# A hybrid attention layer on one core: the dilated heads' output projection moved into the latent stage, its sums passed through DRAM

## Chip, core and metric

One core of one Trainium2 chip. The metric is the device time of one execution in microseconds; the lower the better. Times inside a profiled execution are counted from the start of its span.

## What is computed

One decoder layer on x of 1024 positions by 1024 channels, float32. One input projection gives latent queries and keys, gates, and the dilated heads' q, k and v. Eight latent (MLA) heads of 64 and eight dilated heads of 64 each give a 512-wide output per position; each is multiplied by a SiLU gate. The part that matters here is the end:

```python
y_a = mla_attention(c_q, c_kv, k_rope, q_norm_g, kv_norm_g, w_uq, w_ukv) * jax.nn.silu(g_a)
y_b = dilated_attention(q_b, k_b, v_b) * jax.nn.silu(g_b)
mix = jnp.concatenate([y_a, y_b], axis=-1)
x = layernorm(DEEPNORM_ALPHA * x + mix @ w_out, ln_g, ln_b)
```

`mix @ w_out` contracts 1024 channels: blocks 0 to 3 of 128 are the latent heads' pairs, blocks 4 to 7 the dilated heads' pairs.

## The kernel before

Matrices with float32 precision are split into a high and a low part (`hi_lo`, L74: a ScalarE copy in the matmul's float32 format, then a subtraction on VectorE or GpSimd), and each product takes three passes: high by high, high by low, low by high (`PASSES`, L36). Code is written in program order; a scheduler of the framework orders each engine's queue, and tile pools decide when a buffer is free. Each engine and each DMA queue works through its instructions in that order. Loads, stores and transposing DMAs are issued by SyncE (SP).

The stages, by the time they take place:

1. Input projections, splits and their stores to DRAM (to about 290 us).
2. The dilated heads, pair by pair (L591 to L687), with the gates' matmuls (`gate`, L517) as fillers between them. The gated result of pair j and half s of the positions is the tile `GT[4 + j, s]`, 128 channels by 512 positions.
3. The latent heads (L962 to L1007). The loop runs over 64 units: 4 pairs `hp`, in each 4 chunks `ch` of 256 positions (in the order of `CHS`), 2 heads `e` and 2 blocks `qi` of 128 queries. A unit is: `scores` (L789, three passes of a 128-query block against its 128 to 1024 keys into a PSUM tile S, then VectorE's scale, mask and minimum, L810), `expo` (ScalarE, L815), and three units later `inverse`, `high` (L823: for some widths a scaling on GpSimd, then ScalarE's rounding to f16) and `low` (L835: the rest, on GpSimd or VectorE, and a DMA that transposes the probabilities into PT, L844). Eight units later `values` (L846) multiplies with V and VectorE gates the result into GT (L857). The next pair's keys (`gen_k`, L723) and queries (`gen_q`, L761) are made in between. PSUM: scores have three tiles of two banks; `values`, `gen_k` and `gen_q` share the pool `pb` of two banks (`gbank`, L582).
4. The output projection. `KORD` (L921) is the order of the eight blocks: 0, 1, 4, 5, 6, 7, 2, 3. `load_wo` (L926) loads and splits a block's 128 x 1024 weights, `load_y` (L938) splits the gated results. Blocks 0 and 1 of three rows of 128 positions are begun during pair 3; four more weight blocks (`LATE`, L961) and the rest are loaded around the last units, into buffers of the pools that units use (`b4`, `hp_`). `project` (L948) does 6 matmuls of 512 columns per block and row into PSUM: 48 per row, 384 in all.
5. Row by row `residual` and `finish` (L1036 to L1061), all on VectorE but for one square root: x times ALPHA plus the sum (L1041), statistics (L1044, L1049), 1 / sqrt refined by a Newton step (L1051 to L1056), and two steps with the gain and the shift (L1059, L1060), then the store.

The last stage of a row in the kernel before:

```python
nc.vector.scalar_tensor_tensor(x[:, a:b], x[:, a:b], ALPHA, p[:, a:b], ALU.mult, ALU.add)      # L1041
nc.vector.scalar_tensor_tensor(o, o, mv[:, 0:1], lg[c], ALU.subtract, ALU.mult)                # L1059
nc.vector.scalar_tensor_tensor(o, o, rs[:, 1:2], lb[c], ALU.mult, ALU.add)                     # L1060
```

Line numbers L... are those of the kernel before unless said otherwise; the new code stands some 7 to 50 lines further down (its chunk matmuls are its L986, its residual additions L1084, its shift additions L1111).

## Time and profile before

| what | us |
|---|---|
| median of 3 runs (lowest, highest) | 653.2 (651.88, 655.94) |
| the profiled execution | 648.14 |
| its span, first to last instruction | 646.3 |
| TensorE busy in the span | 594.8 |
| VectorE busy | 398.2 |
| ScalarE busy | 320.0 |
| GpSimd busy | 299.1 |

The span is 1.84 us shorter than the execution's time. Busy times of TensorE count a matmul from its start to its modelled end, and matmuls overlap, so two busy matmuls in a row can stand for less work than the sum of their durations. PEclk in a window is the granted TensorE clock as a share of its higher level (2.4 GHz; the lower, 1.2 GHz, would be 0.50).

### The profile page before, as it was taken

What the parts mean: (1) busy time and instruction counts of PE and PEld (TensorE: products, weight loads), DVE (VectorE), ACT (ScalarE), POOL (GpSimd) and SP (SyncE); (2) the same over time, 40 slices, a digit from 0 to 9 for tenths busy, and PEclk for the clock granted to TensorE, in tenths of its full rate; (3) what the DMA queues carried; (4) which work ended last, traced back from release to release, by engine and by line L of the source; (5) the groups of instructions that cost most, each with busy time, mean ns of one, the idle gap of its engine ahead of it and who ended that gap; (6) DMA issues with size and microseconds to landing.
All of it is one profiled execution on the core that took longest, in us unless ns stands there. A gap on an engine that the chain in (4) does not pass through costs nothing. (4 is left out here: it accounts for less than half of the span.)

```text
span 646.3 us, 11099 instructions
## 1 busy us (share of the span) xinstructions
PE 594.8 (92%) x4046; PEld 435.7 (67%) x4046; DVE 398.2 (62%) x890; ACT 320.0 (50%) x645; POOL 299.1 (46%) x326
## 2 busy tenths in 40 slices
PE   8999998999999899999997987887989977999995
PEld 5888886788999366776764644434545546778884
DVE  3425318480541686644644897678898997365696
ACT  4452136554221386545636575577978787340000
POOL 3374754265331227534644757373758566450000
PEclk9999999999999999999997997988999987999999
DMA  6666137796012779993999996549798899752042
GB/s 198 188 198 198 30 97 204 221 289 174 33 66 74 260 233 144 184 208 78 225 296 234 184 212 147 108 94 185 150 159 163 173 199 225 185 154 81 17 163 98
DMA packets 198663, 105.52 MB, mean 163 GB/s; under 512 B 157520, under 2 KB 175568, under 8 KB 198480
## 3 DMA queue, kind: packets, MB, share of 16 engines
q1 hardware_dynamic: 195008, 99.11, 64.7%
q10 hardware_dynamic: 3600, 5.71, 3.4%
q8 instruction: 31, 0.51, 0.3%
q14 instruction: 24, 0.20, 0.1%
HBM read 47.65 MB, written 18.35 MB: 102 GB/s over the span
## 5 line engine op out<-in xcount | busy, mean ns | idle before, releaser
L522 PE MATMUL gP<-x,wg 128*128 128x512 f32 x384 | 98.8, 406 | 5.9 <-ACT wg L75 5.5
L522 PEld LDWEIGHTS gP<-x,wg 128*128 128x128 f32 x384 | 70.7, 191 | 23.2 <-ACT wg L75 6.1
L953 PE MATMUL op<-wo,ys 128*128 128x512 f32 x288 | 70.7, 401 | 0.6 <-ACT ys L75 0.4
L953 PEld LDWEIGHTS op<-wo,ys 128*128 128x128 f32 x288 | 54.3, 191 | 14.4 <-ACT ys L75 0.9
L815 ACT ACTIVATE p<-p,sm 128x128 f32<-128x128 f32 (+3 forms) x64 | 49.1, 767 | 22.1 <-DVE sm L810 17.3
L804 PE MATMUL S<-k,q 128*128 128x512 f16 (+3 forms) x288 | 54.7, 339 | 5.2 <-DVE sm L810 4.8
L253 PE MATMUL cP<-x,wc 128*128 128x512 f32 x240 | 56.7, 395 | 0.0
L810 DVE CUSTOM_DVE_ANT_0 p<-S,mask,fs 128x128 f32<-128x128 f32 (+3 forms) x64 | 50.5, 809 | 4.7 <-POOL ph L840 3.4
L253 PEld LDWEIGHTS cP<-x,wc 128*128 128x128 f32 x240 | 44.7, 188 | 10.3
L620 ACT ACTIVATE td<-td,st 128x384 f32<-128x384 f32 (+1 forms) x64 | 42.1, 659 | 16.6 <-DVE st L614 16.4
L638 POOL TENSOR_SCALAR td<-td,st 128x384 f32<-128x384 f32 (+1 forms) x32 | 22.5, 710 | 56.9 <-DVE st L626 44.4
L804 PEld LDWEIGHTS <-q 128*128 128x128 f16 x288 | 26.7, 101 | 30.8 <-issue 5.7
L614 DVE CUSTOM_DVE_ANT_0 td<-Sd,mdil,dsc 128x384 f32<-128x384 f32 (+1 forms) x64 | 41.3, 679 | 9.1 <-PE Sd L610 8.9
L168 PE MATMUL acc<-wq,x 128*128 128x512 f32 x192 | 45.1, 395 | 0.9 <-DVE x L155 0.8
L854 PE MATMUL O<-pT,v 128*64 128x256 f16 (+1 forms) x480 | 33.1, 285 | 13.9 <-DMA pT<-ph 11.4
L129 PE MATMUL qkP<-wk,x 128*128 128x512 f32 x192 | 44.5, 393 | 0.0
L840 POOL TENSOR_TENSOR ph<-p,ph 128x256 f16<-128x256 f32 (+3 forms) x32 | 36.6, 1153 | 15.6 <-ACT ph L833 12.4
L854 PEld LDWEIGHTS <-v 128*64 128x64 f16 x480 | 28.8, 119 | 22.1 <-issue 18.4
L842 DVE SCALAR_TENSOR_TENSOR ph<-p,sm,ph 128x128 f16<-128x128 f32 (+3 forms) x32 | 35.0, 1101 | 13.8 <-ACT ph L833 13.8
L168 PEld LDWEIGHTS acc<-wq,x 128*128 128x128 f32 x192 | 36.0, 188 | 10.5 <-DVE x L155 1.3
L129 PEld LDWEIGHTS qkP<-wk,x 128*128 128x128 f32 x192 | 36.0, 188 | 8.2
L653 POOL TENSOR_TENSOR p<-td,p 128x384 f16<-128x384 f32 (+1 forms) x32 | 35.7, 1124 | 11.4 <-ACT p L643 11.2
(313 smaller groups left out, 1158.7 us busy)
## 6 DMA issues: line engine op xcount, KB each, us to landing
u<-in_w_u_dram SPq DMA_DIRECT2D x20, 256.0 KB, 3.1
v_d<-v SPq DMA_DIRECT2D x16, 256.0 KB, 2.1
wor<-in_w_o_dram SPq DMA_DIRECT2D x8, 512.0 KB, 4.2
xr<-in_xres_dram SPq DMA_DIRECT2D x16, 256.0 KB, 3.1
out_dram<-xr SPq DMA_DIRECT2D x16, 256.0 KB, 2.1
xr<-in_xT_dram SPq DMA_DIRECT2D x15, 256.0 KB, 3.0
k_d<-k SPq DMA_DIRECT2D x8, 384.0 KB, 4.4
c_d<-c SPq DMA_DIRECT2D x10, 256.0 KB, 2.4
```

Source lines behind the costliest of these rows:

```text
L129: nc.tensor.matmul(d, xs[k][i // 4][:, a, (i % 4) * P:(i % 4) * P + P], w8[k][:, b, o:o + w], **flags(k, KD, (a, b)))
L168: nc.tensor.matmul(acc[i], xs[k][i // 4][:, a, (i % 4) * P:(i % 4) * P + P], ws[:, b, :512], start=(k == 0 and (a, b) == (0, 0)), stop=(k ...
L253: nc.tensor.matmul(dst, ww(k, a, m), xs[k][s][:, b], **flags(k, KD, (a, b)))
L522: nc.tensor.matmul(p, wg[k // 4][:, a, (k % 4) * P:(k % 4) * P + P], xs[k][s][:, b], **flags(k, KD, (a, b)))
L614: nc.vector.tensor_tensor_reduce(TD[u_][:, e, :ns * P], S[e], mk, dsc[:, 1:2], BIG, ALU.add, ALU.min, stt[:, e, 0:1])
L620: nc.scalar.activation(t[:, :w], t[:, :w], AF.Exp, bias=ST[u_][:, e, 0:1], scale=-1.0, accum_out=ST[u_][:, e, 1:2])
L804: nc.tensor.matmul(S[:, lo:hi], q[:, a, qc], k[:, b, lo:hi], start=((a, b) == (0, 0)), stop=((a, b) == (1, 0)))
L810: nc.vector.tensor_tensor_reduce(t[:, :w], S[:, :w], M["mask"][:, T - w:], fs[:, 7:8], BIG, ALU.add, ALU.min, sm[:, 0:1])
L815: nc.scalar.activation(TT[u][:, :w], TT[u][:, :w], AF.Exp, bias=SM[u][:, 0:1], scale=-1.0, accum_out=SM[u][:, 1:2])
L840: nc.gpsimd.tensor_sub(p16[:, :, 1], t, p16[:, :, 0])
L854: nc.tensor.matmul(O[ME[e], q0:], V[hp][:, kb, vh, ME[e]], rhs, **flags(kb, 2 * ch + 2, (vh, phl)))
L953: nc.tensor.matmul(op[i][:, half(c)], ys[k][a][:, i * P:(i + 1) * P], ws[k][b][:, half(c)], **flags(n_, KD, (a, b)))
```

## The change

- The four dilated blocks of the projection become a generator, `project_dilated`: for each of two halves s of the positions and two halves c of the output columns, four weight pieces of 128 x 512 are loaded (three of the four times), split, and, the first time in s, the gated results too; then for each of four rows 12 matmuls go into one bank of `pb`, a ScalarE copy evicts it, and a store writes it to the DRAM tile `part_d`. That is 16 chunks; each is advanced by half a chunk in two of three units from unit 1 to 47, so beside pairs 0 to 2.
- `KORD` is now 0, 1, 2, 3; blocks 0 to 2 get their weights during pair 3, block 3 after the last unit. Three rows are begun before the last values.
- In the last stage each row's x is multiplied by ALPHA on ScalarE and the stored sum is added on GpSimd (`load_x`); VectorE adds PSUM. For the first five rows the normalisation is one ScalarE instruction (scale and bias), a product with the gain on GpSimd and an addition of the shift on VectorE; the last three rows keep the two steps on VectorE.
- GT tiles are allocated in one place; the second key pair K[1] lies in another pool; new pools `pw` (4), `ph` (5), `pr` (1), `pe` (1) take the room.

```diff
-    KORD = (0, 1, 4, 5, 6, 7, 2, 3)
+    KORD = (0, 1, 2, 3)
...
+        M["pw"], M["ph"], M["pr"], M["pe"] = r("pw", 4), r("ph", 5), r("pr"), r("pe")
...
+    def project_dilated():
+        wd, hi, lo = {}, {}, {}
+        for s, c in ((0, 0), (0, 1), (1, 1), (1, 0)):
+            for j in range(4):
+                if (s, c) != (1, 1):
+                    r = M["pr"].tile([P, 512], F32, name=f"pr{j}{s}{c}", tag="r")
+                    sync.dma_start(r, w_o[4 + j, :, half(c)])
+                    wd[j] = M["pw"].tile([P, 2, 512], F32R, name=f"pw{j}{s}{c}", tag="w")
+                    hi_lo(wd[j][:, 0], wd[j][:, 1], r, nc.gpsimd)
+                if s == c:
+                    g = GT[4 + j, s]
+                    hi[j] = M["ph"].tile([P, 512], F32R, name=f"ph{j}{s}", tag="h")
+                    p_, t_ = (gy, "g") if j + s else (M["ph"], "h")
+                    lo[j] = p_.tile([P, 512], F32R, name=f"pl{j}{s}", tag=t_)
+                    hi_lo(hi[j], lo[j], g, nc.gpsimd)
+            for i in range(4):
+                p = gbank(f"pd{s}{c}{i}")
+                for j in range(4):
+                    for a, b in PASSES:
+                        y = (hi, lo)[a][j]
+                        nc.tensor.matmul(p, y[:, i * P:i * P + P], wd[j][:, b], **flags(j, 4, (a, b)))
+                    if j == 1:
+                        yield
+                t = M["pe"].tile([P, 512], F32, name=f"pe{s}{c}{i}", tag="e")
+                nc.scalar.copy(t, p)
+                sync.dma_start(part_d[4 * s + i, :, half(c)], t)
+                yield
...
-    DR = {3: [0, 1], 5: [2, 3], 7: [4, 5]}
-    NW, NWS, NYS = 2, 4, 3
-    LOADW, LOADY, PROJ0, NY = (3, 8), (5, 8, 10), (13, 15), 3
-    LATE = (NU - 2, NU, NU + 1, NU + 5)
+    DR = {3: [0, 1], 5: [2]}
+    NW, NY = 3, 3
+    LOADW, LOADY, PROJ0 = (3, 5, 8), (5, 8, 10), (13, 15)
+    more = project_dilated()
...
+        if n < 48 and n % 3 or n == 47:
+            next(more, None)
+        if n == NU:
+            load_wo(KORD[3], b4, "b")
...
+    load_y(KORD[3], hp_, "p16")
...
+        t = (b4 if j < 4 else rows).tile([P, T], F32, name=f"row{i}", tag="b" if j < 4 else "row")
+        sync.dma_start(t, part_d[i])
+        for c in range(2):
+            nc.scalar.mul(xr[i][c], xr[i][c], ALPHA)
+            nc.gpsimd.tensor_add(xr[i][c], xr[i][c], t[:, half(c)])
...
-        nc.vector.scalar_tensor_tensor(x[:, a:b], x[:, a:b], ALPHA, p[:, a:b], ALU.mult, ALU.add)
+        nc.vector.tensor_add(x[:, a:b], x[:, a:b], p[:, a:b])
...
+        last = i in ROWS[-3:]
+        if not last:
+            nc.vector.scalar_tensor_tensor(rs[:, 0:1], mv[:, 0:1], -1.0, rs[:, 1:2], ALU.mult, ALU.mult)
...
+                nc.scalar.activation(o, o, AF.Identity, scale=rs[:, 1:2], bias=rs[:, 0:1])
+                nc.gpsimd.tensor_mul(o, o, lg[c])
+                nc.vector.tensor_add(o, o, lb[c])
```

What the new order of instructions is at three places follows. TensorE, pair 1, around the second query projection of head 1 (`qg111`), before: the scores of unit (1, 0, head 1, block 0), then the query projection.

```order
L804 MATMUL S101_5063<-k11_4060,q101_4950 128x128
L804 LDWEIGHTS q101_4950
L804 MATMUL S101_5063<-k11_4060,q101_4950 128x128
L765 LDWEIGHTS u1_4792
L765 MATMUL qg111_5074<-c2_3662,u1_4792 128x512
```

And now: between scores and the same projection stand the last matmuls of two chunks, `pd010` and `pd011`, both of the second group of weights, for their fourth weight piece (`pw301`; `ph30` and `pl30` are the high and low part of the gated result).

```order
L811 LDWEIGHTS q101_5063
L811 MATMUL S121_5345<-k11_4699,q101_5063 128x384
L986 MATMUL pd010_5101<-pw301_5098,ph30_4765 128x512
L986 MATMUL pd011_5200<-pw301_5098,ph30_4765 128x512
L986 MATMUL pd010_5101<-pw301_5098,ph30_4765 128x512
L986 MATMUL pd010_5101<-pw301_5098,pl30_4766 128x512
L986 MATMUL pd011_5200<-pw301_5098,ph30_4765 128x512
L986 MATMUL pd011_5200<-pw301_5098,pl30_4766 128x512
L772 LDWEIGHTS u1_4873
L772 MATMUL qg111_5239<-c2_3666,u1_4873 128x512
```

The query projection has moved behind both chunks, which hold the two banks of `pb` until the fourth piece is there, and the scores have run one chunk further ahead.

GpSimd, around the last low part of the probabilities (`ph301`, on which the last transpose waits), before:

```order
L840 TENSOR_TENSOR ph300_6315<-p310_6268,ph300_6315 128x2x128
L76 TENSOR_TENSOR wo51_6382<-wor5_6379,wo50_6381 128x1024
L840 TENSOR_TENSOR ph301_6392<-p311_6311,ph301_6392 128x2x128
L76 TENSOR_TENSOR wo61_6398<-wor6_6395,wo60_6397 128x1024
L76 TENSOR_TENSOR wo71_6465<-wor7_6462,wo70_6464 128x1024
```

And now:

```order
L838 TENSOR_SCALAR p311_6671<-p311_6671,sm301_6660 128x256
L77 TENSOR_TENSOR wo31_6742<-wor3_6739,wo30_6741 128x1024
L847 TENSOR_TENSOR ph300_6675<-p310_6639,ph300_6675 128x2x128
L1077 TENSOR_TENSOR xr00_6857<-xr00_6857,row0_6861 128x512
L1077 TENSOR_TENSOR xr01_6858<-xr01_6858,row0_6861 128x512
L847 TENSOR_TENSOR ph301_6747<-p311_6671,ph301_6747 128x2x128
L1077 TENSOR_TENSOR xr10_6867<-xr10_6867,row1_6871 128x512
```

Two additions of stored sums (`row0` into `xr00` and `xr01`) stand ahead of the last low part where a weight half stood, and the late weight halves are gone.

VectorE, between the rows' last steps, before:

```order
L1044 BN_STATS bs5_6968<-xr51_6916 128x6
L1056 SCALAR_TENSOR_TENSOR rs4_6903<-rs4_6903 128x1
L1049 BN_AGGR mv5_6973<-bs5_6968 128x2
L1060 SCALAR_TENSOR_TENSOR xr40_6843<-xr40_6843,rs4_6903,lb0_6587 128x512
L1060 SCALAR_TENSOR_TENSOR xr41_6844<-xr41_6844,rs4_6903,lb1_6588 128x512
```

And now:

```order
L1087 BN_STATS bs4_7121<-xr41_7087 128x6
L1111 TENSOR_TENSOR xr10_6867<-xr10_6867,lb0_6851 128x512
L1084 TENSOR_TENSOR xr6_7192<-xr6_7192,op600_7200 128x512
L1111 TENSOR_TENSOR xr11_6868<-xr11_6868,lb1_6852 128x512
L1084 TENSOR_TENSOR xr6_7192<-xr6_7192,op610_7217 128x256
```

The shift additions of an early row (row 1, `lb`) now stand between the residual additions of the last row (row 6), and each waits for GpSimd's product.

## Rows read from the trace of the kernel before

**Rows 1.** Windows: busy us by engine, PEclk, DMA share, GB/s.

```profile
core 0: us, PE busy (x) PEld busy (x) DVE busy (x) ACT busy (x) POOL busy (x), PEclk, DMA share, GB/s
399.40:435.60 36.20, 28.86 (x213) 14.83 (x212) 24.89 (x58) 22.83 (x49) 21.50 (x22) 0.95 0.56 112
435.60:470.20 34.60, 29.31 (x231) 17.16 (x230) 29.72 (x68) 28.43 (x58) 19.80 (x20) 0.95 0.85 164
470.20:503.40 33.20, 29.79 (x241) 17.20 (x240) 29.70 (x68) 26.03 (x53) 23.06 (x21) 1.00 0.89 159
503.40:540.70 37.30, 28.06 (x234) 18.56 (x233) 35.24 (x71) 29.60 (x55) 21.71 (x17) 0.91 1.01 190
540.70:646.30 105.60, 97.32 (x495) 77.92 (x494) 66.81 (x132) 20.40 (x39) 20.85 (x15) 0.97 0.42 129
```

**Rows 2.** Timeline of TensorE, 450 to 480 us: start, length, instructions.

```profile
458.50 1.47 PE L730 MATMUL kg<-c,u 128*128 128x512 f16 x6
...
472.38 1.34 PE L854 MATMUL O<-pT,v 128*64 128x256 f16 x24 [1.48 <-DVE g L857]
473.66 2.12 PE L765 MATMUL qg<-c,u 128*128 128x512 f16 x9
```

**Rows 3.** Groups of TensorE, 399.4 to 540.7: busy us, mean ns, idle before.

```profile
L804 PE MATMUL S<-k,q 128*128 128x512 f16 (+3 forms) x286 | 54.5, 340 | 5.2 <-DVE sm L810 4.8 <-POOL q L771 0.4
L765 PE MATMUL qg<-c,u 128*128 128x512 f16 x118 | 27.8, 379 | 4.4 <-DVE qf L768 4.4
L854 PE MATMUL O<-pT,v 128*64 128x256 f16 (+1 forms) x397 | 27.8, 289 | 13.9 <-DMA pT<-ph 11.4 <-DVE g L857 2.3
L730 PE MATMUL kg<-c,u 128*128 128x512 f16 x36 | 8.8, 379 | 1.8 <-DVE qf L768 1.8
```

**Rows 4.** The chain that ended last, 578 us to the end: start, length.

```profile
591.09 36.25 PE op L953 x158
...
641.40 0.23 DVE rs L1054
...
641.85 0.75 DVE xr L1060
```

**Rows 5.** The page's DMA issues: count, size, median us to landing.

```profile
xr<-in_xres_dram SPq DMA_DIRECT2D x16, 256.0 KB, 3.1
```

**Rows 6.** Groups, 399.4 to 540.7, ScalarE's copies of 512 columns.

```profile
L770 ACT CAST q<-qf 128x512 f16<-128x512 f32 x15 | 9.1, 609 | 5.6 <-DVE qf L768 5.4
```

**Rows 7.** The subtractions of L76: ns lowest/median/highest, first to last us.

```profile
L76 DVE TENSOR_TENSOR ys<-g,ys x16: 677/680/2890, 541.6 to 581.1; 128x512 fp32r<-128x512 f32 x16
...
L76 POOL TENSOR_TENSOR wg<-wg10r,wg x2: 1285/1287/1289, 304.8 to 360.3; 128x512 fp32r<-128x512 f32 x2
```

**Rows 8.** Window of the last rows' matmuls, columns as in rows 1.

```profile
591.00:638.60 47.60, 47.57 (x231) 39.72 (x229) 36.32 (x87) 1.21 (x6) 0.00 (x0) 1.00 0.26 92
```

**Rows 9.** Timeline, 541 to 575 us: the last unit's steps, a meeting.

```profile
537.36 5.15 SPq L844 DMA_TRANSPOSE pT<-ph  x1
...
551.37 0.48 DVE L810 CUSTOM_DVE_ANT_0 p<-S,mask,fs 128x256 f32<-128x256 f32 x1 [3.37 <-POOL ph L840]
...
553.08 0.48 POOL L831 TENSOR_SCALAR p<-p,sm 128x256 f32<-128x256 f32 x1 [1.74 <-DVE sm L821]
...
557.13 0.68 POOL L840 TENSOR_TENSOR ph<-p,ph 128x256 f16<-128x256 f32 x1 [3.57 <-ACT ph L833]
...
568.50 2.40 POOL L76 TENSOR_TENSOR wo<-wor,wo 128x1024 fp32r<-128x1024 f32 x1 [0.99 <-ACT wo L75]
568.98 3.08 DVE L76 TENSOR_TENSOR ys<-g,ys 128x512 fp32r<-128x512 f32 x2 [4.69 <-ACT ys L75]
```

**Rows 10.** Timeline of VectorE, 603 to 612 us, in the last stage.

```profile
603.08 1.28 DVE L1041 SCALAR_TENSOR_TENSOR xr<-xr,op 128x512 f32<-128x512 f32 x2 [8.52 <-PE op L953]
604.29 3.65 DVE L1044 BATCH_NORM_STATS2 bs<-xr 128x6 f32<-128x512 f32 x6
...
610.50 1.41 DVE L1059 SCALAR_TENSOR_TENSOR xr<-xr,mv,lg 128x512 f32<-128x512 f32 x2
```

**Rows 11.** The chain, 455 to 470 us: VectorE's last reading of the key bank.

```profile
464.42 0.76 DVE k L735
```

More of the change, by code (lines that the diff above doesn't have):

```diff
@@ L55, in tile_hybrid_layer @@
     k_d = dpool.tile([T, PAIRS * 3 * P], F16, name="k_d")
+    part_d = dpool.tile([NB, P, T], F32, name="part_d")
     v_d = [dpool.tile([NB, P, PAIRS, 2, P], F16, name=f"v_d{j}") for j in range(2)]
@@ L529, in gate @@
             gate_load(GLOAD[m, s], 1)
-        g = GT[m, s] = gy.tile([P, 512], F32, name=f"g{m}{s}", tag="g")
+        g = GT[m, s]
         nc.scalar.activation(g, p, AF.Tanh, scale=0.5)
@@ L575, in tile_hybrid_layer @@
     gy = left("gy", 2 * KD)
+    for s in range(2):
+        for m in (4, 5, 6, 7):
+            GT[m, s] = gy.tile([P, 512], F32, name=f"g{m}{s}", tag="g")
+    for m in range(4):
+        for s in range(2):
+            GT[m, s] = gy.tile([P, 512], F32, name=f"g{m}{s}", tag="g")
     load_v(0)
@@ L698, in open_latents @@
         lat, M["qf"] = r("lat"), r("qfp")
-        for j in (1, 0):
-            K[j] = [lat.tile([P, 2, T], F16, name=f"k{j}{e}") for e in range(2)]
+        K[0] = [lat.tile([P, 2, T], F16, name=f"k0{e}") for e in range(2)]
+        M["pw"], M["ph"], M["pr"], M["pe"] = r("pw", 4), r("ph", 5), r("pr"), r("pe")
     def load_tab(s, t):
@@ L917, in tile_hybrid_layer @@
     load_tab(1, mm[:, 1].rearrange("p (e c) -> p e c", e=2))
+    K[1] = [b8.tile([P, 2, T], F16, name=f"k1{e}", tag="kk") for e in range(2)]
     for e in range(2):
         gcopy(K[1][e][ME[1 - e]], K[0][e][ME[1 - e]])
-    KORD = (0, 1, 4, 5, 6, 7, 2, 3)
+    KORD = (0, 1, 2, 3)
     stO = ctx.enter_context(ExitStack())
@@ L1007, in tile_hybrid_layer @@
             values(*units[n - VL][:2])
+    load_y(KORD[3], hp_, "p16")
     stT.close()
     l4 = open_pools(ctx)
-    wop, ysp = l4("wop2", 2 * (KD - NW - NWS)), l4("ysp", KD - NY - NYS)
+    rows = l4("rows", 7)
     def halves(name, src):
@@ L1019, in halves @@
         return t
-    for n_, k in enumerate(KORD):
-        if k not in ws:
-            load_wo(k, wop, "wo2")
-        if k not in ys:
-            load_y(k, ysp)
     lg, lb = halves("lg", ln_g), halves("lb", ln_b)
@@ L1028, in tile_hybrid_layer, with load_x @@
         nc.gpsimd.tensor_scalar(g, g, -0.5, 1.0, ALU.mult, ALU.mult)
-    def load_x(i):
-        xr[i] = halves(f"xr{i}", xres[i * P:(i + 1) * P])
     BS = {}
     ROWS, HALVED = (0, 1, 2, 7, 3, 4, 5, 6), (6, 7)
+    def load_x(i):
+        j = ROWS.index(i)
+        if j < 6:
+            xr[i] = halves(f"xr{i}", xres[i * P:(i + 1) * P])
+        else:
+            t = rows.tile([P, T], F32, name=f"xr{i}", tag="row")
+            sync.dma_start(t, xres[i * P:(i + 1) * P])
+            xr[i] = [t[:, half(c)] for c in range(2)]
+        t = (b4 if j < 4 else rows).tile([P, T], F32, name=f"row{i}", tag="b" if j < 4 else "row")
[3 more added lines that the diff above has]
+            nc.gpsimd.tensor_add(xr[i][c], xr[i][c], t[:, half(c)])
     def residual(i, c, p, a, b, n):
@@ L1056, in finish @@
         nc.vector.scalar_tensor_tensor(rs[:, 1:2], rs[:, 0:1], -3.0, rs[:, 1:2], ALU.add, ALU.mult)
+        last = i in ROWS[-3:]
+        if not last:
+            nc.vector.scalar_tensor_tensor(rs[:, 0:1], mv[:, 0:1], -1.0, rs[:, 1:2], ALU.mult, ALU.mult)
         for c in range(2):
             o = xr[i][c]
-            nc.vector.scalar_tensor_tensor(o, o, mv[:, 0:1], lg[c], ALU.subtract, ALU.mult)
-            nc.vector.scalar_tensor_tensor(o, o, rs[:, 1:2], lb[c], ALU.mult, ALU.add)
+            if last:
+                nc.vector.scalar_tensor_tensor(o, o, mv[:, 0:1], lg[c], ALU.subtract, ALU.mult)
+                nc.vector.scalar_tensor_tensor(o, o, rs[:, 1:2], lb[c], ALU.mult, ALU.add)
+            else:
+                nc.scalar.activation(o, o, AF.Identity, scale=rs[:, 1:2], bias=rs[:, 0:1])
+                nc.gpsimd.tensor_mul(o, o, lg[c])
+                nc.vector.tensor_add(o, o, lb[c])
             sync.dma_start(out[i * P:(i + 1) * P, half(c)], o)
@@ L1082, in tile_hybrid_layer @@
                             nc.tensor.matmul(p[:, z[0]:z[1]], ys[k][a][:, i * P:(i + 1) * P],
-                                             ws[k][b][:, c * 512 + z[0]:c * 512 + z[1]], **flags(n_, KD, (a, b)))
+                                             ws[k][b][:, c * 512 + z[0]:c * 512 + z[1]], **flags(n_, PAIRS, (a, b)))
                     residual(i, c, p, *z, n)
```

8 lines of the change are left out of this document (1 added, 7 removed).

## The prediction

> **What bounds the kernel now.** I read the windows by stage first [rows 1]. Four windows run from the first latent scores (399.4 us) to the last unit's scores (540.7 us), and a fifth from there to the end. In the last one TensorE is busy nearly throughout. In the four before it no engine is: VectorE has 0.69 to 0.94 of the window, ScalarE 0.63 to 0.82, and TensorE's busy share, though 0.75 to 0.90, counts each matmul's whole pipelined duration. So I priced TensorE by spacing instead. Nine f16 matmuls of 512 columns take 2.12 us [rows 2]; with a mean duration of 0.379 us [rows 3] that is (2.12 - 0.379) / 8 = 0.218 us from one to the next. The value matmuls come at 1.34 / 24 = 0.056 us [rows 2]. In the last stage 158 f32 matmuls of 512 columns take 36.25 us [rows 4], so 0.229 us each: there the array is simply full.
>
> The stretch from 399.4 to 540.7 lasts 141.3 us. Its matmuls need: scores, 64 units of three passes and 128 to 1024 columns, which is 110,592 columns or 216 times 512, 216 x 0.218 = 47.1 us; queries 118 x 0.218 = 25.7; keys 36 x 0.218 = 7.8; values 397 x 0.056 = 22.2 [rows 3]. That is 102.8 us, so 38.5 us of the stretch are not used. The groups name 5.2 + 4.4 + 13.9 + 1.8 = 25.3 us of this as waits, mostly for the transposing DMA and for VectorE [rows 3]. The rest is short starts and the windows with a granted clock under 1.00 [rows 1]. So a latency-bound stretch stands before a stage bound by TensorE. The change moves matmuls from the second into the first; their number, 384 in the output projection, stays.
>
> **Term 1: the stretch.** It gains 16 chunks of 12 matmuls, 192 x 0.229 = 44.0 us, and by the new order 18 matmuls of row 0's projection that stood later, 4.1 us: 48.1 us in all. If the chunks fill all 38.5 unused us, the stretch grows by 9.6; if they fill the 25.3 us of named waits, by 22.8; if they fill nothing, by 48.1. I take the middle of the ends, 29 us, which leaves TensorE at (102.8 + 48.1) / 170.3 = 0.89 of the stretch against 0.73 before. Two things keep it from 9.6. Chunks stand at fixed places in TensorE's queue, and a wait elsewhere is not filled. And they bring waits of their own: the weights of a chunk group come through one raw buffer, so each of its four pieces needs a load (3.1 us from issue to landing for 256 KB [rows 5]), a ScalarE copy (0.61 us [rows 6]) and a GpSimd subtraction (1.29 us [rows 7]), 5 us, before the next is loaded: 20 us for a group, twice in the stretch.
>
> The rest of what the stretch gains I cost at nothing, under cover. ScalarE gets 36 more instructions (12 weight halves, 8 gated halves, 16 evictions), 36 x 0.61 = 22 us on top of 107 busy us [rows 1]: 129 of 170. GpSimd gets 20 subtractions of 1.29 us, 26 us on top of 86: 112. The DMA queues get 28 transfers of 256 KB, 7.3 MB. While plain transfers alone ran, 92 GB/s cost a share of 0.26 [rows 8], so 354 GB/s at a full share and 21 us for these; the stretch had a mean share of 0.83 [rows 1], 117 us, and 138 of 170 is 0.81. If the chunks filled everything and the stretch stayed near 151 us, DMA at 0.91 and ScalarE at 0.85 would be late next, which is one more reason for the middle. What queues behind a chunk that waits: on TensorE the next scores or query projection, on ScalarE behind an eviction the exponentials, on SP behind a store of sums the transposes of the probabilities.
>
> **Term 2: from the last scores to the end, 105.6 us before [rows 1].** In the kernel before, the last units' buffers are shared with late weights and split outputs, and the last small unit's mask-and-minimum runs at 551.37, ten us after its scores [rows 9]. The change asks for its last weights later in the program and has one split output left there, so I let that wait go. From there: scores to the scaled row 2.2 us; on GpSimd a weight half of 2.40, a low part of 0.68, two additions of stored sums at 1.29, the last low part of 0.68, 6.3 us [rows 7, 9]; a transpose 5.2 [rows 9]; values and gate 1. That is 15 us. Then 30 matmuls of the f32 form (24 for row 7, six for row 0's last block) stand before row 0's sum is whole: 30 x 0.229 = 6.9 us.
>
> From there 96 matmuls of 512 columns and 24 of 256, at half of 0.229, are left, 25 us of TensorE, and VectorE is the longer one. Its work by the new order: 15 residual additions at 1.28 / 2 = 0.64 us, 9.6; two of half the width at an estimated two thirds of that, 0.9; 14 statistics at 3.65 / 6 = 0.61, 8.5; four of half the width, by the same estimate, 1.6; 45 small instructions at 0.2, 9.0 [rows 4, 10]; ten additions of the shift, which the trace has as VectorE's addition of two SBUF tiles at 0.68, 6.8 [rows 7]; and for the last three rows 12 old-form steps at 1.41 / 2 = 0.70, 8.4 [rows 10]. With rounding that is 45 us. Before, 32 such steps took 22.4 us, but beside matmuls (36.25 us in one run of 158) that hid most of them; now the cover is shorter than VectorE's work, so moving five rows' normalisation to three engines (-14 + 6.8 + 1 us on VectorE) only lessens what becomes the bound.
>
> GpSimd gets 16 additions and 10 products here, 26 x 1.29 = 34 us. They meet VectorE. At 568.50 GpSimd starts a subtraction of 2.40 us; two VectorE subtractions that start at 568.98 and would take 2 x 0.68 = 1.36 us take 3.08 [rows 7, 9]. So a VectorE instruction with two SBUF inputs waited for the GpSimd one. I expect eight of the 22 such instructions to meet one, at half of 1.29 each: 5 us (bounds: 0, and 22 x 1.29 = 28).
>
> The Trainium skill ("SBUF — State Buffer", section "Who interferes with whom") says that VectorE and GpSimd share a port pair by an exclusive lock, and that the loser waits for the whole instruction; the trace agrees at 568.50. By that rule alone every one of the 22 that falls on a GpSimd instruction waits, which is the third rival's price.
>
> The end after VectorE's last pair stays: 646.3 - 641.85 - 1.41 = 3.0 us [rows 4, 10]. Term 2 is 15 + 6.9 + 45 + 5 + 3.0 = 74.9 us, 30.7 less than before.
>
> **The sum.** 29 - 30.7 = -1.7 us: a span of 644.6 us, and with the 1.84 us around it 646.4 us against 648.14 of the profiled execution. The runs' median is 653.2, 1.0078 times that execution, so 651 us.
>
> **Rivals.** (1) The chunks fill nearly every wait: the stretch grows by 14, not 29. For it: 25.3 us are named waits, and a chunk needs nothing that scores make. Against: fixed places, two banks. Span 629.6, so 631.4 and 636 us in the runs' measure: faster.
>
> (2) PSUM banks. Chunks take banks from the pool of two that keys, queries and values use. Six key matmuls of 1.47 us held theirs from 458.50 until VectorE's reading ended at 465.18, 6.7 us [rows 2, 11]. The new order has both banks held by chunks whose fourth weight is awaited, with a query projection behind them. If a group's 20 us of weights are not covered by the matmuls placed among them, TensorE stands, and the chunks come on top of the old waits: growth 45, span 660.6, 668 us: slower. It decides from about 36 us of growth on, and needs both group changes to stall.
>
> (3) GpSimd's products and VectorE's two-input instructions exclude each other throughout the last stage: 28 us, not 5. Span 667.6, 675 us: slower. Against: most of GpSimd's 16 additions run before VectorE starts, and the residual additions read one input from PSUM.
>
> **How the numbers follow.** A measurement of this kernel tells about 1% from no change. Forecast 0.42 (651 us, its own range 647 to 659), rival 1 0.35, rival 2 0.15, rival 3 0.08. So faster 0.35, same 0.42, slower 0.23. The range takes in rival 1 with two us to spare and ends just above rival 2: 634 to 670.
>
> **What would show it.** Right: the stretch up to the last unit's scores is 165 to 175 us, TensorE's waits for the DMA there are mostly gone, TensorE ends 15 to 25 us before the span does, and VectorE has hardly a gap over the last 50 us. Wrong on term 1: a stretch under 160 us (rival 1) or over 180 with TensorE waiting for weight pieces or banks (rival 2). Wrong on term 2: last scores to end far from 75 us, or shift additions of over 1.3 us (rival 3).

## The result, and the profile after

The changed kernel takes 677.12 us (median of four runs, 674.72 to 680.98), the kernel before beside it 654.55 us (651.88 to 655.94): a ratio of 1.0355, 95% interval 1.0293 to 1.0418. It is slower by 3.5%; 651 us was forecast, and the range ended at 670. The four runs of the kernel after lie 6.3 us apart, so the times of single runs below say little by themselves, and the text goes by the stages of one profiled execution each. Its profiled execution took 674.72 us with a span of 672.9, against 646.3 before.

The windows of the kernel after, cut at the first scores of each pair, at the last unit's scores and at the end, as in [rows 1]:

```profile
core 0: us, PE busy (x) PEld busy (x) DVE busy (x) ACT busy (x) POOL busy (x), PEclk, DMA share, GB/s
403.50:446.20 42.70, 41.24 (x289) 25.17 (x287) 25.37 (x58) 26.65 (x57) 26.31 (x27) 0.99 0.71 145
446.20:493.20 47.00, 41.10 (x266) 24.77 (x262) 32.60 (x72) 34.78 (x69) 26.54 (x27) 0.96 0.75 169
493.20:550.00 56.80, 50.65 (x315) 31.69 (x312) 32.71 (x70) 35.64 (x69) 26.27 (x26) 0.94 0.63 135
550.00:594.90 44.90, 35.76 (x275) 22.63 (x271) 34.15 (x63) 32.14 (x59) 24.27 (x18) 0.92 1.08 241
594.90:672.90 78.00, 49.15 (x277) 40.15 (x274) 48.70 (x117) 20.11 (x42) 44.48 (x37) 0.86 0.53 162
```

Read it against [rows 1] by stage. The first three pairs, beside which 15 of the 16 chunks run (the last one falls into the start of the last pair, at 553.8), went from 104.0 to 146.5 us (+42.5), the last pair from 37.3 to 44.9 (+7.6); the stretch of term 1 so grew by 50.1 us, where 29 was forecast. The last stage fell from 105.6 to 78.0 (-27.6, forecast -30.7). The first latent scores come 4.1 us later. 4.1 + 50.1 - 27.6 = 26.6, the difference of the spans.

Now TensorE's column. Before, it was busy 28.86 + 29.31 + 29.79 = 88.0 of the first 104.0 us, so 16.0 us were idle. After, it is busy 133.0 of 146.5: 45.0 us more in the column, for chunk matmuls of 180 x 0.229 = 41.2 us, and 13.5 us idle. The chunks were added, and next to none of the idle time went. The granted clock does not explain it: 0.99, 0.96 and 0.94 in these three windows, 0.95, 0.95 and 1.00 before.

TensorE's groups from 403.5 to 594.9 us, columns as in [rows 3]:

```profile
L811 PE MATMUL S<-k,q 128*128 128x512 f16 (+3 forms) x285 | 54.0, 331 | 6.7 <-DVE sm L817 4.1 <-POOL q L778 2.4
L986 PE MATMUL pd<-pw,ph 128*128 128x512 f32 x128 | 45.3, 427 | 6.2 <-POOL pw L77 2.5 <-DVE qf L775 2.0 <-ACT pe L990 0.9
L772 PE MATMUL qg<-c,u 128*128 128x512 f16 x127 | 33.1, 409 | 1.5 <-ACT pe L990 1.1 <-DVE k L742 0.3
L861 PE MATMUL O<-pT,v 128*64 128x256 f16 (+1 forms) x396 | 25.9, 284 | 6.5 <-DMA pT<-ph 5.3 <-DVE k L742 1.0 <-PE pd L986 0.3
```

The values' wait for the transposing DMA fell from 11.4 to 5.3 us and the queries' wait from 4.4 to 1.5, as a filler should do. But the chunks wait 6.2 us themselves, for weight pieces (`pw`) and for banks (`qf`, `pe`). These four groups wait 20.9 us; the four of [rows 3] waited 25.3.

Three stages per run carry the rest of this text (us; the stretch of an expectation is the first three pairs and the last pair together, to within 0.5 us):

| kernel | first scores at | first three pairs | last pair | last stage | span |
|---|---|---|---|---|---|
| before | 399.4 | 104.0 | 37.3 | 105.6 | 646.3 |
| after | 403.5 | 146.5 | 44.9 | 78.0 | 672.9 |
| e1 no chunks | 402.8 | 109.2 | 43.6 | 73.0 | 628.6 |
| e2 weights once | 402.0 | 136.2 | 44.3 | 80.3 | 662.8 |
| e3 one pass | 405.4 | 138.9 | 43.8 | 77.7 | 665.8 |
| e4 off ScalarE | 403.2 | 151.2 | 43.6 | 79.2 | 677.2 |
| e5 own banks | 403.4 | 143.5 | 47.5 | 79.3 | 673.7 |
| e6 two score tiles, no chunks | 402.7 | 107.0 | 42.1 | 81.9 | 633.7 |
| e7 whole chunks | 410.9 | 144.9 | 44.0 | 79.0 | 678.8 |
| e8 no matmuls | 409.7 | 116.4 | 43.0 | 82.4 | 651.5 |
| e9 one pass, own banks | 403.6 | 127.7 | 46.0 | 77.1 | 654.4 |
| e10 four banks (before) | 401.8 | 119.0 | 31.8 | 107.7 | 660.3 |
| e11 norm alone (before) | 399.0 | 103.3 | 37.4 | 107.3 | 647.0 |
| e12 norm on VectorE (after) | 403.4 | 146.7 | 44.2 | 80.8 | 675.1 |
| e13 half the chunks | 403.8 | 131.1 | 43.3 | 74.5 | 652.7 |
| e14 half, at half the rate | 403.6 | 124.2 | 46.1 | 75.3 | 649.2 |
| e15 no chunks, third block late | 402.0 | 107.2 | 40.3 | 79.6 | 629.1 |
| e16 no chunks, old key place | 400.0 | 107.7 | 38.5 | 83.2 | 629.4 |

How far two executions of the same code differ can be read here too: e11 has the latent stage of before, and e12 that of after, and their first three pairs agree with them to 0.7 and 0.2 us. e7 and e8 are 6 to 7 us late before the latent stage begins, where neither differs from the kernel after, so stages are compared here, not spans.

### The profile page after: what moved, and what is told of

Its sections match the earlier page's. It is cut to its first block, busy times and chain, and to the rows that moved or that the text cites. A ratio compares the mean times of both kernels' runs of the same rounds, so it can differ in the third digit from the quotient of the medians.

```text
span 672.9 us, 11203 instructions
## 1 busy us (share of the span) xinstructions
PE 598.7 (89%) x4034; PEld 433.3 (64%) x4034; DVE 386.2 (57%) x877; ACT 346.5 (51%) x694; POOL 347.9 (52%) x369
## 5 line engine op out<-in xcount | busy, mean ns | idle before, releaser
L254 PEld LDWEIGHTS cP<-x,wc 128*128 128x128 f32 x240 | 44.8, 188 | 10.3
L986 PE MATMUL pd<-pw,ph 128*128 128x512 f32 x128 | 45.3, 427 | 6.2 <-POOL pw L77 2.5
L645 POOL TENSOR_SCALAR td<-td,st 128x384 f32<-128x384 f32 (+1 forms) x32 | 21.5, 679 | 52.0 <-DVE st L633 42.1
L621 DVE CUSTOM_DVE_ANT_0 td<-Sd,mdil,dsc 128x384 f32<-128x384 f32 (+1 forms) x64 | 41.5, 679 | 11.2 <-PE Sd L617 10.9
L849 DVE SCALAR_TENSOR_TENSOR ph<-p,sm,ph 128x128 f16<-128x128 f32 (+3 forms) x32 | 33.1, 1049 | 24.0 <-ACT ph L840 24.0
L811 PEld LDWEIGHTS <-q 128*128 128x128 f16 x288 | 24.8, 99 | 34.0 <-issue 11.8
L838 POOL TENSOR_SCALAR p<-p,sm 128x256 f32<-128x256 f32 (+3 forms) x32 | 22.4, 710 | 41.3 <-DVE sm L828 38.6
L861 PE MATMUL O<-pT,v 128*64 128x256 f16 (+1 forms) x480 | 32.6, 289 | 12.1 <-DMA pT<-ph 10.9
L772 PE MATMUL qg<-c,u 128*128 128x512 f16 x144 | 37.9, 414 | 4.1 <-DVE qf L775 2.6
```

Source lines behind the costliest of these rows:

```text
L254: nc.tensor.matmul(dst, ww(k, a, m), xs[k][s][:, b], **flags(k, KD, (a, b)))
L621: nc.vector.tensor_tensor_reduce(TD[u_][:, e, :ns * P], S[e], mk, dsc[:, 1:2], BIG, ALU.add, ALU.min, stt[:, e, 0:1])
L772: nc.tensor.matmul(p, U[hp][:, a, (3 * e + k) * P:(3 * e + k) * P + P], M["c"][2 + k][:, b, half(s)], **flags(k, 3, (a, b)))
L811: nc.tensor.matmul(S[:, lo:hi], q[:, a, qc], k[:, b, lo:hi], start=((a, b) == (0, 0)), stop=((a, b) == (1, 0)))
L861: nc.tensor.matmul(O[ME[e], q0:], V[hp][:, kb, vh, ME[e]], rhs, **flags(kb, 2 * ch + 2, (vh, phl)))
L986: nc.tensor.matmul(p, y[:, i * P:i * P + P], wd[j][:, b], **flags(j, 4, (a, b)))
```

## The experiments

Theory A: the chunks stand at fixed places in TensorE's queue, and their matmul time adds to the stretch. Theory B: not the matmuls, but the weight pieces and evictions on ScalarE, GpSimd and the DMA queues slow the units.

**e1: no chunks.** The dilated heads' half of the projection is left out, and the residual is read a second time in place of the stored sums.

```diff
-    more = project_dilated()
+    more = iter(())
```

> The changed kernel without its 16 chunks: the dilated heads' half of the projection is left out, and x is read in place of the stored sums. Theory A (the chunks' matmuls add their own time, because they stand at fixed places in TensorE's queue ahead of matmuls that others wait for) and theory B (the chunks' weight pieces and evictions hold ScalarE's queue and TensorE) both expect the stretch from the first latent scores to the last unit's scores back at 141 to 147 us, from 191.9, and the last stage unchanged at 75 to 79 us, so a span near 625. A third theory, that new pools and buffer places and not the chunks lengthen the stretch, expects it above 160.

630.39 us, before beside it 656.39. Windows of its four pairs:

```profile
402.80:442.00 39.20, 29.12 (x212) 15.64 (x211) 24.34 (x60) 23.34 (x52) 20.52 (x23) 0.96 0.58 118
442.00:479.70 37.70, 31.10 (x231) 18.12 (x230) 30.91 (x65) 28.09 (x56) 20.43 (x21) 0.91 0.77 154
479.70:512.00 32.30, 29.70 (x241) 17.18 (x240) 28.78 (x66) 26.67 (x54) 23.03 (x22) 1.00 0.92 165
512.00:555.80 43.80, 32.78 (x254) 21.19 (x252) 39.01 (x75) 33.21 (x60) 23.32 (x18) 0.88 0.90 183
```

The chunks cost the first three pairs 37.3 us. But 5.2 us of growth there and 6.3 in the last pair stay without any chunk, more than was expected: the stretch is 152.8 us, between the 141 to 147 of theories A and B and the 160 of the third.

**e2: weights once.** The pieces of the first group serve all groups (the products for other columns are then those of the first).

```diff
-                if (s, c) != (1, 1):
+                if (s, c) == (0, 0):
```

> The changed kernel with the first group's weight pieces used by all four groups: eight loads, copies and subtractions of weight pieces are left out (the second column half is computed with the first half's weights), all 192 matmuls stay. Theory A: stretch 183 to 192 us. Theory B: the weight pieces are the larger part of the growth, stretch 175 us or less.

664.83 us; first three pairs 136.2, so reloading costs 10.3 of the 37.3 us: a part, not the whole. The stretch of 180.5 us lies between the two forecasts.

**e3: one pass.** One of three passes per chunk, 64 matmuls instead of 192; only the product of the high parts is left.

```diff
-                    for a, b in PASSES:
-                        y = (hi, lo)[a][j]
-                        nc.tensor.matmul(p, y[:, i * P:i * P + P], wd[j][:, b], **flags(j, 4, (a, b)))
+                    nc.tensor.matmul(p, hi[j][:, i * P:i * P + P], wd[j][:, 0], start=j == 0, stop=j == 3)
```

> The changed kernel with one pass in place of three in the chunks: 64 matmuls instead of 192 (the low-part products are left out), loads, copies, subtractions, evictions and stores all stay. Theory A: growth falls to about a third, stretch 155 to 163 us. Theory B: stretch 175 us or more.

667.85 us; first three pairs 138.9. Two thirds of the matmuls gone and only 7.6 us with them: theory A in its plain form falls, and the stretch of 182.7 us is where theory B had it.

**e4: off ScalarE.** Weight copies on GpSimd, evictions on VectorE.

```diff
-                    hi_lo(wd[j][:, 0], wd[j][:, 1], r, nc.gpsimd)
+                    hi_lo_g(wd[j][:, 0], wd[j][:, 1], r)
...
-                nc.scalar.copy(t, p)
+                nc.vector.tensor_copy(t, p)
```

> The changed kernel with the chunks' copies taken off ScalarE: the high parts of weights and gated results on GpSimd, the evictions on VectorE. Theory A: stretch within 5 us of 191.9. Theory B (ScalarE's queue held by chunk work): 182 us or less.

678.98 us; first three pairs 151.2, 4.7 more, and the stretch of 194.8 us is within theory A's 5 us. So ScalarE's queue alone is not the cause. The run does not show its part to be nothing: the pieces now come from GpSimd, and the chunks wait 7.9 + 3.0 = 10.9 us for them, where they waited 2.5:

```profile
L986 PE MATMUL pd<-pw,ph 128*128 128x512 f32 x120 | 42.0, 424 | 13.5 <-POOL pw L84 7.9 <-POOL pw L80 3.0 <-DVE qf L775 1.5
```

That left theory C, the mechanism of rival 2: chunks hold the two banks of `pb` that keys, queries and values need.

**e5: own banks**, and its control **e6**. The chunks get the two banks of the third score tile, which opens only in the last pair; e6 has the same two score tiles and no chunks. More banks also let the scheduler place queries and keys earlier, so the order on TensorE is not quite the same.

```diff
-    SB[1] = open_pools(ctx, space=PSUM)("ps_b")
+    pc = open_pools(stC, space=PSUM)("pc", 2)
...
-                p = gbank(f"pd{s}{c}{i}")
+                p = pc.tile([P, 512], F32, name=f"pd{s}{c}{i}", tag="c")
```

> The chunks get two PSUM banks of their own (those of the third score tile, which is opened only when the chunks are done, so that the scores of the first three pairs share two tiles instead of three). The rest is the kernel after. To be read against the next run, which has the same two score tiles and no chunks. Theory C (the chunks hold the two banks that keys, queries and values need, and these then come late): the stretch from the first latent scores to the last grows by 20 us or less over that of the run without chunks; bubbles of the chunks stay, but queries and values no longer wait for a bank. Theory A' (the chunks' matmuls stand in TensorE's queue in front of scores and values, and their waits for weights hold the engine itself): it grows by 30 us or more, as in the kernel after (38.6 us).

> Control of the run with own banks: two score tiles instead of three for the first three pairs, and no chunks (their sums are left out; the residual is read a second time in their place). If a third score tile is of no use there, the stretch is 153 us as in the run without chunks; if it is, 160 to 175 us. Both theories take it only as the base line.

675.48 and 635.48 us. First three pairs of e5:

```profile
403.40:454.80 51.40, 48.61 (x308) 29.29 (x307) 26.95 (x64) 30.42 (x61) 29.52 (x29) 0.95 0.69 145
454.80:498.20 43.40, 43.36 (x295) 26.20 (x294) 30.28 (x66) 32.38 (x66) 25.75 (x26) 1.00 0.88 195
498.20:546.90 48.70, 46.20 (x310) 27.88 (x306) 31.94 (x69) 32.22 (x65) 23.49 (x24) 1.00 0.73 165
```

and of e6:

```profile
402.70:438.80 36.10, 32.13 (x245) 16.78 (x243) 26.45 (x65) 26.76 (x55) 23.91 (x25) 0.95 0.78 153
438.80:473.80 35.00, 29.46 (x231) 16.46 (x231) 27.48 (x67) 27.54 (x57) 17.66 (x19) 0.95 0.88 167
473.80:509.70 35.90, 31.90 (x239) 16.99 (x238) 29.43 (x66) 27.10 (x55) 23.43 (x22) 0.95 0.78 153
```

The chunks cost 143.5 - 107.0 = 36.5 us with banks of their own, as many as without, and 191.0 - 149.1 = 41.9 over the stretch, against 38.6 without: theory C falls as the cause of the loss. (By e6's stretch of 149.1 us a third score tile is of no use there.) The middle row of e5 shows what is left: TensorE is busy 43.36 of 43.40 us. Its idle time fell from 13.5 (e6) to 5.3 us over the three pairs; the chunks do fill waits now, and the stretch is as long as that of the kernel after (191.0 against 191.4), because there was so little to fill.

**e7: whole chunks.** All 12 matmuls of a chunk at one step, in every third unit.

```diff
-                    if j == 1:
-                        yield
...
-        if n < 48 and n % 3 or n == 47:
+        if n < 48 and n % 3 == 1 or n == 47:
```

> A chunk's 12 matmuls are issued at one step (every third unit) instead of half at one and half at the next, so its bank is not held across a unit of scores. Theory C: the mean hold of a bank falls from 7.0 us to 3 to 5 us and the stretch from 191.6 to 170 to 183 us. Theory A': the same work in the same queue, in lumps of 2.75 us that delay the scores behind them more: 190 to 200 us.

680.64 us; first three pairs 144.9, 1.6 less than after, and the stretch 188.9: neither the gain of theory C nor a loss. Shorter holds of the banks do not help either.

**e8: no matmuls.** Loads, splits, ScalarE copies and stores stay, the 192 matmuls go.

```diff
-                nc.scalar.copy(t, p)
+                nc.scalar.copy(t, wd[i][:, 0])
```

> The chunks keep their weight loads, their splits, the copy on ScalarE (from a weight tile in SBUF) and the stores; only their 192 matmuls and so their PSUM tiles are left out. Theories A' and C: the stretch falls to 153 to 163 us, close to the run without chunks. Theory B (loads, splits and copies on ScalarE, GpSimd and the DMA queues slow the units' own work): it stays above 175 us.

653.36 us; first three pairs 116.4, and the stretch of 159.4 us is where theories A' and C had it.

```profile
409.70:450.90 41.20, 32.10 (x222) 16.29 (x221) 23.31 (x54) 28.22 (x62) 29.74 (x31) 0.91 0.79 198
450.90:489.10 38.20, 31.14 (x232) 16.89 (x230) 32.53 (x70) 31.53 (x63) 22.55 (x23) 0.87 0.98 204
489.10:526.10 37.00, 28.37 (x231) 16.52 (x230) 31.69 (x66) 31.02 (x62) 24.59 (x24) 1.00 1.03 199
```

So the matmuls are worth 30.1 us there and everything else of the chunks 7.2 over e1; with e2's 10.3, 7 to 10 us for the pieces. How much falls to which depends a little on the order in which one adds them, and e8 had a lower granted clock in the first two pairs than e1 (0.91 and 0.87 against 0.96 and 0.91), so 7.2 may be too much. Theory B is a fifth to somewhat over a quarter of the cost.

**e9: one pass and own banks**, to settle e3.

> One of the three passes of each chunk (64 of the 192 matmuls; the dilated heads' half of the product is then only its leading part) and own PSUM banks for the chunks, i.e. the run with one pass and the run with own banks put together. The question is why a third of the matmuls with shared banks made the first three pairs only 7.6 us shorter (138.9 us against 146.5). Theory C' (two ceilings: with all passes TensorE is full, with one pass the shared banks are the bound): the first three pairs take 107 us (two tiles, no chunks) + 15 us of matmuls or less, 107 to 124 us. Theory W (the chunks' waits for their weight pieces and splits hold TensorE's queue, whatever the banks): 130 to 140 us, as with one pass alone.

656.26 us; first three pairs 127.7, 11.2 less than e3, and near 107.0 (e6) + 7.2 (pieces) + 64 x 0.229 = 128.9. It lies between the two forecasts, and theory C' had left out the pieces. The first three pairs of e3:

```profile
405.40:440.50 35.10, 30.24 (x227) 16.88 (x226) 22.26 (x54) 22.60 (x51) 23.41 (x25) 1.00 0.72 151
440.50:492.40 51.90, 37.22 (x240) 20.68 (x238) 34.95 (x78) 40.79 (x79) 32.38 (x30) 0.89 0.84 193
492.40:544.30 51.90, 40.94 (x276) 24.00 (x276) 32.14 (x69) 32.44 (x65) 24.03 (x24) 0.91 0.65 147
```

and of e9:

```profile
403.60:447.40 43.80, 39.10 (x275) 22.06 (x273) 25.91 (x62) 28.71 (x59) 28.41 (x29) 0.96 0.65 149
447.40:485.50 38.10, 34.77 (x244) 19.49 (x244) 29.32 (x67) 32.08 (x66) 27.57 (x26) 0.96 1.05 217
485.50:531.30 45.80, 39.36 (x272) 21.68 (x271) 30.74 (x71) 34.64 (x71) 24.01 (x24) 0.96 0.95 202
```

TensorE's idle time falls from 30.5 us to 14.5, so with a third of the matmuls shared banks do cost some 11 us, or 9.0 over the stretch (182.7 to 173.7), of which e6 gains 3.7 over e1 without any chunk. With all of them TensorE is nearly full once banks are free, and banks no longer matter. That is why e3 and e5, each alone, gained so little. The theory that is left is A with a ceiling: the chunks' matmuls fill a part of what TensorE has idle beside them, a good 10 us (24.8 idle in e8, 13.5 in the kernel after), and the rest of them adds.

**e10: four banks for the kernel before**, without any chunk, with two score tiles in the first three pairs.

```diff
-        return pb.tile([P, 512], F32, name=name, tag="g")
+        GB.append(GB.pop(0))
+        return GB[-1].tile([P, 512], F32, name=name, tag="g")
...
-    SB[1] = open_pools(ctx, space=PSUM)("ps_b")
+    GB.append(open_pools(stC, space=PSUM)("pc", 2))
```

> The kernel before, without any part of the change, in which keys, queries and values take turns over four PSUM banks instead of two for the first three pairs; the third score tile, whose banks they are, is opened for the last pair. In the stretch of the kernel before, TensorE waited 8.5 us for the reader of a bank (queries 4.4, keys 1.8, values 2.3 us). Bank theory: these go, the stretch is 133 to 138 us instead of 141.5 and the time 645 to 651 us. Theory that the units' chain (VectorE 85% busy, ScalarE 76%) sets the pace: the stretch stays within 140 to 145 us and the time within 1% of before.

663.19 us (661.51 to 666.47), ratio 1.0142 (1.0074 to 1.0209): slower by some 1.4%, and the stretch of 150.8 us is what neither theory forecast. Its first groups, 401.8 to 552.6 us:

```profile
L807 PE MATMUL S<-k,q 128*128 128x512 f16 (+3 forms) x285 | 56.0, 334 | 11.8 <-DVE sm L813 10.0 <-POOL q L774 1.8
L768 PE MATMUL qg<-c,u 128*128 128x512 f16 x118 | 32.8, 427 | 1.4 <-DVE qf L771 1.4
L857 PE MATMUL O<-pT,v 128*64 128x256 f16 (+1 forms) x397 | 28.8, 277 | 15.8 <-DMA pT<-ph 15.8
```

The bank waits of [rows 3] went (queries 4.4 to 1.4, values' 2.3 to nothing) and came back elsewhere: the scores wait 10.0 us for VectorE's reading of a score tile instead of most of 5.2, the values 15.8 us for transposes instead of 11.4. With four banks the scheduler also set the keys of pair 2 to the start of pair 1 (439.2 and 440.8, its first scores 439.0), where before they came 14 and 23 us after it, and there is a score tile less, so this run tells of banks, score tiles and order together; it is no gain either way.

**e11: the norm alone**, in the kernel before: five rows on three engines.

```diff
+            if not last:
+                nc.scalar.activation(o, o, AF.Identity, scale=rs[:, 1:2], bias=rs[:, 0:1])
+                nc.gpsimd.tensor_mul(o, o, lg[c])
+                nc.vector.tensor_add(o, o, lb[c])
```

> The kernel before with one part of the change alone: the norm of the first five row tiles on ScalarE, GpSimd and VectorE instead of VectorE alone. In the tail of before TensorE's matmuls run to 638.6 of 646.3 us and VectorE waits for them (15.4 us at the line that adds the sums), so the VectorE time saved (20 operations of 0.74 us become 10 of 0.74 to 0.87) is cover that nothing needs: within 0.5% of before, tail 104 to 107 us. The rival of the prediction (GpSimd and VectorE shut each other out): 3 to 6 us slower.

652.66 us (ten runs), ratio 1.0009 (0.9967 to 1.0051): no difference. Its last stage is 107.3 us, just over what was expected.

**e12: the norm back on VectorE**, in the kernel after.

```diff
-        last = i in ROWS[-3:]
+        last = True
```

> The kernel after with that part undone: all norms on VectorE, the rest as changed. Tail of after 77.8 us with VectorE busy 48.7 us. Twenty operations of 0.744 us instead of ten of 0.87 us are 6.2 us more on VectorE. If VectorE sets the end of the tail: 82 to 85 us. If TensorE's matmuls and the loads do: 77 to 79 us.

677.25 us, last stage 80.8: 2.8 us more, between the two cases, while the time lies within the runs of the kernel after (674.72 to 680.98). VectorE's busy time there rose only from 48.70 to 51.94 us: its steps with gain and shift cost 5.8 us more, near the 6.2 forecast, but three of its small steps (L1097, L1099, L1102) cost 2.3 less.

**e13 and e14: half the chunks**, at the full and at half the rate (row tiles 4 to 7 lack the dilated heads' part).

```diff
-        for s, c in ((0, 0), (0, 1), (1, 1), (1, 0)):
+        for s, c in ((0, 0), (0, 1)):
...
-        if n < 48 and n % 3 or n == 47:
+        if n < 48 and n % 3 == 1 or n == 47:
```

> Only the first 8 of the 16 chunks (row tiles 0 to 3; for row tiles 4 to 7 the dilated heads' part is left out and the residual read in its place), at the same rate, so that they are done after 24 of the first 48 units. Without chunks the first three pairs took 109.2 us (104.0 in before), with 16 chunks 146.5. No room at all: half of the 37.3 us, 125 to 131 us. Room for a few: 8 chunks are 22 us of matmuls, of which most of the 16 us of idle TensorE time would be filled, 110 to 120 us.

> The same 8 chunks at half the rate (one half of a chunk in every third unit), over all 48 units. No room at all: 125 to 131 us for the first three pairs, as at the full rate. Density theory (a chunk does harm because it stands in two units of three, so that the units' chain never catches up): 8 us or more under the run at the full rate, 110 to 120 us.

654.54 and 651.35 us. First three pairs 131.1: 8 chunks cost 21.9 us over e1, 2.74 each, pieces included, and 12 x 0.229 = 2.75. The first chunks are not cheaper than the last (15.4 us for the other seven in the first three pairs, 2.2 each); there is next to no room at that rate, and TensorE is idle for 17.2 us, where e1 had 19.3. At half the rate they cost 15.0, 1.9 each, and the idle time is 13.5. That is just below "no room" (124.2, where 125 to 131 was forecast), so spreading helps, by less than the density theory wanted.

**e15 and e16: the 11.5 us that stay without chunks.** Both are e1 with one thing more. e15 loads the third latent weight block at the end of the last pair; e16 puts the second key buffer back and leaves out the chunks' buffers.

```diff
-    LOADW, LOADY, PROJ0 = (3, 5, 8), (5, 8, 10), (13, 15)
+    LOADW, LOADY, PROJ0 = (3, 8), (5, 8, 10), (13, 15)
```

```diff
-    K[1] = [b8.tile([P, 2, T], F16, name=f"k1{e}", tag="kk") for e in range(2)]
```

> The run without chunks (the dilated heads' half left out, the residual read in its place), with the third latent weight block loaded where the kernel before loads its third, at the end of the last pair, instead of in its middle. If this block's load, copies and GpSimd subtraction, and the six matmuls of row 0 that follow it, cost the last pair its growth: the last pair falls from 43.8 us to 37 to 40 us (before: 37.5) and the stretch from 153.0 to 147 to 150 us; the tail may gain 2 to 4 us. If it is the rest of the last pair's order: 42 to 45 us.

> The run without chunks, with the second key buffer again beside the first (in the kernel after it takes a place that the last dilated pair frees) and without the chunks' buffers in SBUF. If the place of the keys delays the first three pairs: these fall from 109.2 us to 104 to 106 us (before: 104.0). If not: 108 to 110 us.

630.87 and 631.29 us. In e15 the last pair falls to 40.3 us, about as forecast; in e16 the first three pairs fall by 1.5 us only, but the last pair to 38.5 and the start to 400.0. In both the last stage takes back what the pairs give (79.6 and 83.2 against 73.0), and the spans are 629.1, 629.4 and 628.6. So these 11.5 us seem to be mostly no loss: work moves across the line at the last unit's scores, and the end stays. What part of the order moves it was not traced further.

## Why the prediction was wrong

**The step that failed is term 1: "if they fill the 25.3 us of named waits ... if they fill nothing, by 48.1. I take the middle of the ends, 29 us".** It grew by 50.1, more than the end at which nothing is filled. The miss of 21.1 us can be split by e1 and e8:

| part of term 1 | forecast | measured |
|---|---|---|
| the chunks' matmuls, first three pairs | 24.9 | 30.1 (e8 to after) |
| pieces, splits, evictions, stores | 0, "under cover" | 7.2 (e1 to e8) |
| first three pairs without chunks | 0 | 5.2 (before to e1) |
| last pair | 4.1 | 7.6 |

The first three pairs hold 180 of the 192 matmuls; the other 12 are in the last pair's 7.6. Three things went wrong in it.

*The room was too large.* I set aside TensorE's busy column because a matmul's duration exceeds its spacing, priced TensorE by spacing, and called 38.5 us unused. But the chunks run only beside the first three pairs, and there the windows had 16.0 us idle; 9.2 of the named 25.3 lay in the last pair. The other 13.2 (116.0 busy less 102.8 priced) was TensorE busy: 3.0 of it in 78 matmuls of the dilated heads that the sum left out (L686, two groups of 1.5 us), the rest at a slower pace than was priced. The chunks found no room in that: with them the busy column rose by 45.0 for 41.2 us of work. With the right room the ends were 48.1 - 16.0 = 32.1 and 48.1, and their middle, 40, would have given 663 us by the prediction's own sum, still short. The Trainium skill ("Perfetto Trace Analysis", section "Identifying Performance Opportunities") says that TensorE's matmul busy share is no good measure of its distance to the roofline, and points to the share of peak arithmetic and the weight loads' busy share instead. By that the first three pairs had half of TensorE left, (14.83 + 17.16 + 17.20) / 104.0 = 0.47. As a measure of what a filler could still use, the runs bear the busy column out: e5 reached 43.36 of 43.40 with the weight loads' column at 26.20 of 43.40.

*"The rest ... I cost at nothing, under cover."* The busy sums on ScalarE, GpSimd and the DMA queues came out near the forecast (ScalarE 129.2 against 129, GpSimd 103.4 against 112), and beside the chunks none of these was full (DMA share 0.63 to 0.75 in the first three pairs; in the last pair it was 1.08). Yet the pieces cost 7 to 10 us. A part of that shows as chunk and unit waiting for each other in order: `pd` 2.5 us for `pw` and 0.9 for `pe`, queries 1.1 for `pe`; the rest was not traced.

*The stages are not separate.* e15 and e16 show up to 10 us crossing the line between the two terms at an unchanged end, so a forecast of one term to a few us says less than it seems.

**Term 2 came out near.** 78.0 us against 74.9, though two errors in it partly cancel: 7.3 us too little up to the last values, 4.2 too much after row 0's sum. VectorE is the longer engine; from 624.1 to the end it is busy 42.95 us, where 45 of work and 5 of meetings were forecast:

```profile
624.10:672.90 48.80, 26.42 (x126) 21.84 (x125) 42.95 (x102) 12.73 (x24) 24.83 (x19) 0.84 0.30 118
```

TensorE ends 20.7 us before the span (15 to 25 forecast). The end of the chain in the kernel after (start, length):

```profile
602.24 2.37 POOL wo L77
...
605.25 1.24 POOL xr L1077
606.65 1.54 SPq L851
608.24 5.57 DMA pT<-ph
613.86 3.36 PE O L861 x30
617.22 6.88 PE op L1133 x24
624.10 9.58 PE op L961 x42
...
655.29 2.95 DVE xr L1106 x2
```

The values end at 617.2, 22.3 us after the last scores, where 15 was forecast: the last unit's scaling ended at 602.3, 7.4 us after its scores and not 2.2 (ScalarE's rounding ahead of it had waited 2.95 us for a transpose), and the values took 3.36, where 1 was allowed with the gate. GpSimd's part and the transpose came out near the forecast. The 24 matmuls then take 6.88 (6.9 forecast for 30; the granted clock was 0.82 there), and from 624.1 to the end it is 48.8, where 45 + 5 + 3 = 53 was forecast.

**Rival 3** (GpSimd against VectorE) is there at a small size. VectorE's groups in the last stage:

```profile
L1111 DVE TENSOR_TENSOR xr<-xr,lb 128x512 f32<-128x512 f32 x10 | 8.6, 870 | 0.0
L1106 DVE SCALAR_TENSOR_TENSOR xr<-xr,mv,lg 128x512 f32<-128x512 f32 x6 | 5.9, 1010 | 0.0
L1107 DVE SCALAR_TENSOR_TENSOR xr<-xr,rs,lb 128x512 f32<-128x512 f32 x6 | 4.1, 746 | 0.0
```

The shift additions take 870 ns instead of 680 [rows 7], the first of the old steps 1010 instead of 705 [rows 10]: 10 x 0.19 + 6 x 0.305 = 3.7 us, where 5 was taken and 28 was the rival's. Its 675 us came nearest to the measured 677.12, but by luck: the loss is not in the last stage.

**Rival 2** (banks, 668 us) was nearest in the stretch, 45 us of growth, and had 0.15, but its mechanism did not bring it: the chunks' waits for pieces and banks sum to 6.2 us, banks alone are worth nothing with all chunks (e5), and some 11 us only when the matmuls are thinned (e9). **Rival 1** (636 us, 0.35) was the worst placed chance: its condition, nearly all waits filled, could not have given its price, since TensorE's busy column over the four pairs rose from 116.0 to 168.8 us, which alone is 27 us more than the old stretch of 141.3, where 14 was its price.

**Why it loses as a whole.** Taking the dilated half out of the last stage is worth 646.3 - 628.6 = 17.7 us of span (before to e1, so with the rest of the change), not its 44.0 us of matmuls; most of VectorE's work there, 42.95 us in the kernel after, has to be done anyway. The profiled execution of before (648.14) is a fast one: against the runs beside e1 and e15 the same step is worth 656.39 - 630.39 = 26.0 and 653.98 - 630.87 = 23.1 us. Beside the pairs the same matmuls and their pieces cost 672.9 - 628.6 = 44.3. Among the kernels that do the whole work, none that was run is faster than the kernel before by more than its interval. A mix, with a few chunks widely spaced and the rest left in the last stage, was not tried as a whole. By e14 (8 chunks for 15.0 us) and half of 17.7 to 26.0 it would, by estimate, come out behind by 2 to 6 us; e14 itself, which leaves the other half out, took 651.35 us, the kernel before beside it 650.15.

## What to carry to other kernels

Before work is moved into another stage's waits, take the idle time of the engine's own busy column in just the windows where the work will stand; that was the bound here, and time in which the engine was busy at a slow pace was no room. Price the move with two leave-out runs, one without the work at the old place and one without it at the new: here the same matmuls were worth 18 to 26 us where they were (the first run here had the rest of the change in it) and 44.3 where they went. And when thinning the work and widening the buffer each gain little, try both together before either theory is dropped: two ceilings of nearly the same height hide each other.
